# Two chunks per product in the small GLA levels of a hybrid GLA and mLSTM decoder layer on one core

## The chip, the cores and the metric

The kernel runs on one core of a Trainium2 chip. The metric is the device time of one execution in microseconds (us). Most executions of this kernel lie within some tenths of a per cent of each other. Every duration, wait and clock below is read from one profiled execution of the kernel before.

## What is computed

One decoder layer: a norm, a wide input projection, four heads of gated linear attention (GLA) beside four heads of mLSTM, a merge by sigmoid gates, an output projection, and a convolutional feed-forward network. Sequence 1024 with 16 meta tokens in front, model width 1024, float32 throughout. The change touches the scores of the GLA heads. Per head (key width 128, value width 256):

```python
def step(S, inp):
    qc, kc, vc, la = inp
    bc = jnp.cumsum(la, axis=-2)
    inter = jnp.einsum('bhtk,bhkv->bhtv', qc * jnp.exp(bc), S)
    diff = bc[:, :, :, None, :] - bc[:, :, None, :, :]
    decay = jnp.exp(jnp.where(causal[:, :, None], diff, -jnp.inf))
    scores = jnp.einsum('bhtk,bhsk,bhtsk->bhts', qc, kc, decay)
    out = inter + jnp.einsum('bhts,bhsv->bhtv', scores, vc)
```

The decay differs per key channel, so the scores are no plain product of queries and keys.

## The kernel before, in words

**Main stream.** TensorE spends the first half of the span on projections of the normed input. They are made as float32r products in three terms (high by high, high by low, low by high): `proj_cm` (L146, matmuls on L154) gives channel-major thirds of 24 matmuls with 342 to 348 columns, `proj_v` (L172, matmuls on L184 and L197) gives the values of a head in nine pieces with 256 columns. Each third or piece ends in a `yield`. The generators are run by `main` in a fixed order, slot by slot: in slot s, the gates of head s (`gate_proj`, six thirds), then keys, queries and values of head s+1 (`head_proj`, three thirds, three thirds, nine pieces), then a merge gate (`merge_gate`, three thirds). A slot has 24 yields.

**Side stream.** The attention of a head is a generator too (`gla(s)` for heads 0 to 3, `mlstm(s)` for 4 to 7). At each yield of the main stream, `advance` runs the side stream one step. So one third of a projection (some 3.8 us of TensorE) stands between two steps, and the side work of ScalarE, VectorE and GpSimd runs under it. The side generators wait in one list and are run one after the other. `small_rows` (seven steps; it makes the small vectors that the mLSTM heads need) stands behind GLA head 0 in that list. A GLA head has 23 steps. A tile scheduler then sets the exact order of instructions on each engine, so a step's instructions can stand some way ahead of the step; each engine runs its own instructions strictly in that order.

**Scores by levels.** A chunk is 128 tokens, and there are NC = 8 chunks. Pairs of a query at t and a key at s in one chunk are split by the largest block of size b (1, 2, 4, ..., 64) that separates them: s lies in the earlier half of an aligned block of 2b tokens, t in the later half. For such pairs the decay factors at the border between the halves, and one matmul makes the level. `level(b)` (L610) builds `pk`: for earlier tokens the key times exp(border - bc), for later tokens the query times exp(bc - border). VectorE does the two subtractions (L624, L625) and the query product (L628), ScalarE the exp (L626), GpSimd the key product (L627).

- Levels 32 and 64 (`scores_pair`, L567) are packed: earlier halves of two chunks in 128 columns, later halves in another 128, and one matmul of 128 by 128 serves two chunks; four matmuls a level.
- Levels 1 to 16 (`scores_later`, L580) take one matmul per chunk: all 128 tokens stationary, the 64 later tokens moving; eight matmuls of 128 by 64 a level. `copy_predicated` (L589) then writes the valid entries into `A` by a mask.
- The diagonal (`scores`, L559) is eight matmuls of 128 by 128, in the head's first step.

These products are plain float32; each shows in the trace as two matmul records, so eight matmuls are 16 records. `A` (128 by 8 by 128) then meets the values on L720; L721 adds the state's part.

**What a head ends with.** `post` (L510) scales the rows, transposes them in groups of four (`ot`, L530, and a group for the two meta rows, `otm`, L537), multiplies by the gate into the row tile `of` (L532, L538), splits it in high and low, and sends both to DRAM. It does this for two halves of the head, and `of` has one buffer: the second half's first write waits until the first half's low part has left.

**Buffers that set the order.** PSUM tiles with tag `s` have three buffers, used in turn by all side products (scores `sc`, `pre`, `ot`, `otm`, `kt`); tag `pj` has three for the projections. Gate tiles `r` have two buffers, one head's worth. Keys `k`, queries `q`, values `v` have two each. `raw_s` (small projections) shares its one buffer with `mfs`, in which GpSimd builds the masks (L365 to L369).

Of the kernel before, what the change touches and what calls it, by code (L numbers as in the profile page):

```python
# [1 line left out]

# [14 lines left out]
P = 128  # L17
# [27 lines left out]
def hybrid_kernel(ctx, tc, x, meta, norm_mix, w_in, b_in, gla_w_gate, gla_b_gate, gla_norm,  # L45
# [167 lines left out]
    def head_units(s):  # L213
        h = s % 4
        if s < 4:
            uk[s], uq[s] = u_cm(w_in, O_GK + P * h, f"gk{h}"), u_cm(w_in, O_GQ + P * h, f"gq{h}")
            if s == 0:
                uk["lr"] = U.add()
            uv[s] = u_v(O_GV + DV * h, f"gv{h}_")
        else:  # L220
            uk[s], uq[s] = u_cm(w_in, O_MK + P * h, f"mk{h}"), u_cm(w_in, O_MQ + P * h, f"mq{h}")
            uv[s] = u_v(O_MV + DV * h, f"mv{h}_")
# [7 lines left out]
    for s in range(8):  # L230
        gate_units(s)
# [127 lines left out]
    with tc.issue_after(last.ins):  # L359
        lmask = {}  # L360
        mfs = hd.tile([P, T], F32, name="mfs", tag="raw", bufs=1)
        for i, b in enumerate((16, 8, 4, 2, 1)):
            mf = mfs[:, 64 * i:64 * (i + 1)]
            half = mf.rearrange("p (n w) -> p n w", w=b)
            nc.gpsimd.memset(half, 1.0)  # L365
            nb = P // (2 * b)
            nc.gpsimd.affine_select(out=half, in_=half, compare_op=OP.is_ge, fill=0.0, base=0,
                                    pattern=[[-2 * b, nb], [0, b]], channel_multiplier=1)
            nc.gpsimd.affine_select(out=half, in_=half, compare_op=OP.is_ge, fill=0.0, base=b - 1,  # L369
                                    pattern=[[2 * b, nb], [0, b]], channel_multiplier=-1)  # L370
            mu = hd.tile([P, 64], U8, name=f"mu{b}")
            nc.vector.tensor_copy(mu, mf)
            lmask[b] = mu
        mu = hd.tile([P, P], U8, name="mu0")
        nc.vector.tensor_copy(mu, ident)
        lmask[0] = mu
        big = hd.tile([P, P], F32, name="big")
# [173 lines left out]
    def gla(s):  # L551
# [7 lines left out]
        def scores(lt, rt, b):  # L559
            for g in range(2):  # L560
                pt = ps.tile([P, 4, P], F32, name=f"sc{s}_{b}_{g}", tag="s", bufs=3)
                for i in range(4):
                    c = 4 * g + i
                    nc.tensor.matmul(pt[:, i, :], lt[:, P * c:P * (c + 1)], rt[:, P * c:P * (c + 1)], start=True, stop=True)
                nc.vector.copy_predicated(A[:, 4 * g:4 * g + 4, :], lmask[b][:, None, :].to_broadcast([P, 4, P]), pt)

        def scores_pair(pk, b):  # L567

            m = 64 // b
# [3 lines left out]
            A2 = A.rearrange("p (i c) t -> p i c t", c=2)  # L573
            for c in range(2):
                for n in range(m):
                    p0 = b * (m * c + n)
                    nc.scalar.activation(A2[2 * b * n:2 * b * n + b, :, c, 2 * b * n + b:2 * b * (n + 1)],
                                         pt[p0:p0 + b, :, p0:p0 + b], AF.Copy)

        def scores_later(pk, b):  # L580

            n = P // (2 * b)
            pt = ps.tile([P, NC, 64], F32, name=f"sc{s}_{b}", tag="s", bufs=3)
            for c in range(NC):
                l = lv(pk[:, P * c:P * (c + 1)], b)[:, :, 1, :]
                nc.tensor.matmul(pt[:, c, :], pk[:, P * c:P * (c + 1)], l, start=True, stop=True)
# [23 lines left out]
        def level(b):  # L610
            pk = wtile(f"pk{s}_{b}")
            n = SEQ // (2 * b)
            if b < 32:
# [822 lines left out]
```

## Time and profile before

| what | value |
|---|---|
| median of 3 runs | 1971.62 us (1969.85 to 1973.77) |
| the profiled execution | 1973.3 us, of which the span is 1971.4 us |
| TensorE busy with matmuls | 1936.3 us, 98% of the span |
| VectorE, ScalarE, GpSimd busy | 963.4, 744.3, 286.5 us |
| mean granted TensorE clock | 0.996 |

How to read the rows below: PE is TensorE, PEld its weight load, DVE VectorE, ACT ScalarE, POOL GpSimd, SP the engine that issues the transfers. L597 is line 597 of the program before. A timeline row gives the start in us, the duration in us (of a merged run of xN records, from the first start to the last end), the engine, line, operation, the output tile, the inputs and the shapes; in brackets the engine's idle time before it and what ended that. Matmuls are pipelined, so a record's own duration (0.32 us) is longer than the distance from one start to the next (0.16 us), and only starts tell what one costs.

### The profile page before, as it was taken

How to read it: one execution, taken by the hardware profiler on the slowest of the kernel's cores; microseconds unless marked ns; L12 is line 12 of the kernel's file. 1: busy time of each engine (PE TensorE's matmuls, PEld its weight loads, DVE VectorE, ACT ScalarE, POOL GpSimd, SP SyncE). 2: the span in 40 equal slices, each digit the busy share in tenths (PEclk: the TensorE clock that was granted, in tenths of full speed). 3: DMA queues.
4: the chain of work that ended last, by engine and by line, in shares of the span. 5: the costliest groups of instructions: out<-in, count | busy, mean ns of one | idle time of the engine just before them, and what ended most of it. 6: DMA issues, size and time to landing. Idle time of an engine off the chain costs nothing. (4 is left out here: it accounts for less than half of the span.)

```text
span 1971.4 us, 31346 instructions
## 1 busy us (share of the span) xinstructions
PE 1936.3 (98%) x13333; PEld 1854.0 (94%) x13333; DVE 963.4 (49%) x1427; ACT 744.3 (38%) x1176; POOL 286.5 (15%) x201
## 2 busy tenths in 40 slices
PE   7999999999999999999999999999999999999998
PEld 6999999999999999999999999999999999978886
DVE  6265263637535343422022446698888888710202
ACT  5145333535534343423221234544545444431211
POOL 2020020101000000000000002012222222364220
PEclk9999999999999999999999999999999999999999
DMA  4210403232234222226971433333333333487731
GB/s 152 57 33 23 100 22 95 37 70 69 61 96 90 64 88 63 79 62 123 315 268 54 150 108 108 124 102 126 116 119 123 118 118 113 170 301 263 239 101 43
DMA packets 191271, 224.82 MB, mean 114 GB/s; under 512 B 11102, under 2 KB 150640, under 8 KB 191131
## 3 DMA queue, kind: packets, MB, share of 16 engines
q1 hardware_dynamic: 190843, 221.76, 37.2%
q8 instruction: 105, 1.72, 0.4%
q10 hardware_dynamic: 288, 1.05, 0.1%
q14 instruction: 35, 0.29, 0.0%
HBM read 166.07 MB, written 56.71 MB: 113 GB/s over the span
## 5 line engine op out<-in xcount | busy, mean ns | idle before, releaser
L1323 PE MATMUL pd<-ringH,a 128*128 128x512 f32 x416 | 131.6, 393 | 1.5 <-DMA a<-adrL 1.5
L154 PE MATMUL pj<-xH,wH_r 128*128 128x342 f32 x384 | 124.2, 323 | 0.4 <-ACT r L426 0.4
L154 PE MATMUL pj<-xH,wL_r 128*128 128x342 f32 x384 | 122.9, 320 | 0.0
L154 PE MATMUL pj<-xL,wH_r 128*128 128x342 f32 x384 | 122.5, 319 | 0.0
L1357 DVE TENSOR_TENSOR acc<-pd,acc 128x512 f32<-128x512 f32 x16 | 11.1, 692 | 196.3 <-PE pd L1323 196.3
L1323 PEld LDWEIGHTS pd<-ringH,a 128*128 128x128 f32 x416 | 78.0, 188 | 19.6 <-DMA a<-adrL 2.0
L1323 PE MATMUL pd<-ringL,a 128*128 128x512 f32 x208 | 82.5, 397 | 1.5 <-POOL ringL L1302 1.5
L197 PE MATMUL pv<-wH_gv,xH 128*128 128x256 f32 x256 | 75.4, 294 | 0.0
L197 PE MATMUL pv<-wH_mv,xH 128*128 128x256 f32 x256 | 74.2, 290 | 0.0
L1193 PE MATMUL po<-wL_wo,yH 128*128 128x256 f32 x256 | 72.0, 282 | 2.0 <-DVE wL_wo L103 2.0
L1193 PE MATMUL po<-wH_wo,yH 128*128 128x256 f32 x256 | 72.8, 284 | 0.9 <-DVE h L1200 0.9
L154 PEld LDWEIGHTS pj<-xH,wH_r 128*128 128x128 f32 x384 | 72.2, 188 | 1.1 <-ACT r L426 0.5
L627 POOL TENSOR_TENSOR pk<-pk,kT 128x512 f32<-128x512 f32 x24 | 40.2, 1685 | 226.9 <-ACT pk L626 226.8
L197 PE MATMUL pv<-wL_gv,xH 128*128 128x256 f32 x256 | 72.7, 284 | 0.0
L197 PE MATMUL pv<-wH_gv,xL 128*128 128x256 f32 x256 | 72.6, 283 | 0.0
L154 PEld LDWEIGHTS pj<-xL,wH_r 128*128 128x128 f32 x384 | 72.2, 188 | 0.0
L154 PEld LDWEIGHTS pj<-xH,wL_r 128*128 128x128 f32 x384 | 72.2, 188 | 0.0
L197 PE MATMUL pv<-wL_mv,xH 128*128 128x256 f32 x256 | 71.9, 281 | 0.0
L197 PE MATMUL pv<-wH_mv,xL 128*128 128x256 f32 x256 | 71.9, 281 | 0.0
L1193 PE MATMUL po<-wH_wo,yL 128*128 128x256 f32 x256 | 71.8, 281 | 0.0
L1154 DVE SCALAR_TENSOR_TENSOR cv<-u,fc,cv 128x1024 f32<-128x1024 f32 x44 | 69.4, 1578 | 0.4
L201 DVE TENSOR_TENSOR v<-pv,bB 128x256 f32<-128x256 f32 x64 | 27.0, 421 | 78.1 <-PE pv L197 77.9
(618 smaller groups left out, 6714.5 us busy)
## 6 DMA issues: line engine op xcount, KB each, us to landing
rd<-in_ffn_w_down_dram SPq DMA_DIRECT2D x36, 512.0 KB, 5.9
rg<-in_ffn_w_up_dram SPq DMA_DIRECT2D x22, 512.0 KB, 4.2
ru<-in_ffn_w_up_dram SPq DMA_DIRECT2D x22, 512.0 KB, 3.8
a<-adrH SPq DMA_DIRECT2D x44, 256.0 KB, 5.0
a<-adrL SPq DMA_DIRECT2D x44, 256.0 KB, 4.7
adrH<-aH SPq DMA_DIRECT2D x21, 512.0 KB, 2.6
adrL<-aL SPq DMA_DIRECT2D x21, 512.0 KB, 2.6
wr_r<-in_w_in_dram SPq DMA_DIRECT2D x16, 512.0 KB, 4.0
```

Of the source, the lines that this page charges most:

```text
L154: nc.tensor.matmul(pt[:, :n], a[:, k, :], b[:, k, base + t0:base + t0 + n], start=(i == 0), stop=(i == 3 * NK - 1))
L197: nc.tensor.matmul(pt[:, :DV], a[:, k, t0:t0 + P], b[:, k % 4, :], start=(i == 0), stop=(i == 3 * NK - 1))
L201: nc.vector.tensor_tensor(vt[:n, c, :DV], pt[:n, :DV], bB[:n, :], OP.add)
L627: nc.gpsimd.tensor_tensor(pe, pe, lv(kv, b)[:, :, 0, :], OP.mult)
L1154: nc.vector.scalar_tensor_tensor(y, u[:, j:SEQ + j], fc[:, j, jj:jj + 1], y, OP.mult, OP.add)
L1193: nc.tensor.matmul(pt[:, :DV], a, b[:, k % 4, :], start=(k == 0 and i == 0), stop=(k == NK - 1 and i == len(terms) - 1))
L1323: nc.tensor.matmul(pts[t][n], a[:, c], b[:, 512 * n:512 * n + 512], start=start and i == 0, stop=stop and i == 2)
L1357: nc.vector.tensor_tensor(acc[:, h], pts[t][n], acc[:, h], OP.add)
```

## The change

- Levels 1 to 16 are packed as levels 32 and 64 are: two chunks to a matmul, four matmuls of 128 by 128 a level (`products`, `scores_small`) where eight of 128 by 64 stood. In a product of two chunks only the two diagonal quarters are wanted. So that both can be written straight over the later columns of the two chunks, the odd chunk's earlier rows are put into `pk` in mirrored order; with that, the scores of an odd chunk come out with their rows mirrored, in the same `A`.
- In `level(b)` for b under 32, the subtraction for the earlier tokens and the key product are each made in two instructions of 256 columns (even chunks; odd chunks mirrored) instead of one of 512.
- `turn` brings the odd chunks' rows back: one float32 matmul with a mirrored identity `flip` (128 by 512 columns), and one ScalarE copy into a new tile `An`. `An` takes the buffer of tag `oH`. It stands two steps behind level 16.
- The diagonal moves from the head's first step to the step of level 32's scores, behind `turn`, since `turn` overwrites whole rows. A GLA head has 24 steps: one fewer at its start, two more at level 64.
- Masks: 22 `affine_select` on GpSimd for the level masks and `flip` where 10 stood (one more, for `big`, is in both), five masks of 128 by 128 where five of 128 by 64 stood, and the tile `flip`.
- Order: for s below 5, the six thirds of keys and queries of head s+1 come ahead of the six gate thirds of head s; the weights are prepared in that order too. `small_rows` is put behind GLA head 3 instead of head 0.

```diff
+    GATE_LATER = [s < 5 for s in range(8)]
...
+        nc.gpsimd.memset(mfs[:, :P * 6], 1.0)
...
+        for i, b in enumerate((16, 8, 4, 2, 1)):
+            mf = mfs[:, P * (i + 1):P * (i + 2)]
+            nb = P // (2 * b)
+            for odd in range(2):
+                half = mf[:, 64 * odd:64 * odd + 64].rearrange("p (n w) -> p n w", w=b)
+                for base, sg in (((P - 1) * odd, -1), (b - 1 - (P - 1) * odd, 1)):
+                    nc.gpsimd.affine_select(out=half, in_=half, compare_op=OP.is_ge, fill=0.0, base=base,
...
+        def turn():
+
+            pt = ps.tile([P, 4, P], F32, name=f"sct{s}", tag="s", bufs=3)
+            nc.tensor.matmul(pt, flip, A.rearrange("p (i c) t -> p i c t", c=2)[:, :, 1, :], start=True, stop=True)
+            nc.scalar.activation(An, pt, AF.Copy)
+
+        def products(pk, b):
+
             pt = ps.tile([P, 4, P], F32, name=f"sc{s}_{b}", tag="s", bufs=3)
             for i in range(4):
                 nc.tensor.matmul(pt[:, i, :], pk[:, P * i:P * (i + 1)], pk[:, 512 + P * i:512 + P * (i + 1)], start=True, stop=True)
-            A2 = A.rearrange("p (i c) t -> p i c t", c=2)
+            return pt
...
-        def scores_later(pk, b):
-
-            n = P // (2 * b)
-            pt = ps.tile([P, NC, 64], F32, name=f"sc{s}_{b}", tag="s", bufs=3)
-            for c in range(NC):
-                l = lv(pk[:, P * c:P * (c + 1)], b)[:, :, 1, :]
-                nc.tensor.matmul(pt[:, c, :], pk[:, P * c:P * (c + 1)], l, start=True, stop=True)
-            dst = A.rearrange("p c (n h w) -> p c n h w", h=2, w=b)[:, :, :, 1, :]
-            m = lmask[b].rearrange("p (n w) -> p n w", w=b)[:, None].to_broadcast([P, NC, n, b])
-            nc.vector.copy_predicated(dst, m, pt.rearrange("p c (n w) -> p c n w", w=b))
-
-        scores(kv, qv, 0)
-        yield
+        def scores_small(pk, b):
+            pt = products(pk, b)
+            dst = A.rearrange("p (i c) (n h w) -> p i (c n) h w", c=2, h=2, w=b)[:, :, :, 1, :]
+            m = lmask[b].rearrange("p (n w) -> p n w", w=b)[:, None].to_broadcast([P, 4, P // b, b])
+            nc.vector.copy_predicated(dst, m, pt.rearrange("p i (n w) -> p i n w", w=b))
...
+                e = pk[:, :512].rearrange("p (i n h w) -> p i n h w", n=64 // b, h=2, w=b)
+                pe = [e[:, :, :, 0, :], e[:, :, ::-1, 1, ::-1]]
...
-                nc.vector.tensor_tensor(pe, ref, b4[:, :, 0, :], OP.subtract)
+                for e, _, t in early:
+                    nc.vector.tensor_tensor(e, t[..., b - 1:b].to_broadcast(t.shape), t, OP.subtract)
...
-                nc.gpsimd.tensor_tensor(pe, pe, lv(kv, b)[:, :, 0, :], OP.mult)
+                for e, k, _ in early:
+                    nc.gpsimd.tensor_tensor(e, e, k, OP.mult)
...
             if b == 64:
-                scores_pair(pk, 32)
+                yield
+                turn()
+                yield
+                scores_diagonal()
+                scores_large(pk, 32)
...
-                nc.tensor.matmul(op[:, i, :], A[:, c, :], vt[:, c + 1, :DV], start=True, stop=False)
+                nc.tensor.matmul(op[:, i, :], Ac[c], vt[:, c + 1, :DV], start=True, stop=False)
...
-        if s == 0:
+        if s == 3:
             side.append(small_rows())
+        nxt = head_proj(s + 1) if s < 7 else iter(())
+        if GATE_LATER[s]:
+            main(islice(nxt, 6))
         main(gate_proj(s))
-        if s < 7:
-            main(head_proj(s + 1))
+        main(nxt)
         main(merge_gate("a", s))
```

Three places show how the order of instructions moves. The rows name line, operation, output and inputs, and columns (or partitions by columns); xN is a run of N like instructions.

TensorE in slot 0 around level 2 of head 0 (`sc_2`); `pj` are projection matmuls, `gk`, `gq` and `r` the weights of keys, queries and gates. Before:

```order
L154 MATMUL pj_684_1181<-xL,wH_r_1_749 128x342
L154 MATMUL pj_684_1181<-xH,wL_r_1_750 128x342
L586 MATMUL sc_2_1213<-pk_2_1165 128x64 x8
L154 MATMUL pj_0_1233<-xH,wH_gk_991 128x348
L154 MATMUL pj_0_1233<-xL,wH_gk_991 128x348
```

The same place in the changed kernel:

```order
L155 MATMUL pj_342_1155<-xL,wH_gq_759 128x342
L155 MATMUL pj_342_1155<-xH,wL_gq_760 128x342
L600 MATMUL sc_2_1189<-pk_2_1141 128x128 x4
L155 MATMUL pj_684_1195<-xH,wH_gq_759 128x342
L155 MATMUL pj_684_1195<-xL,wH_gq_759 128x342
```

Four matmuls of 128 columns stand where eight of 64 stood, and they stand under the queries of head 1 and no longer at the end of the gates of head 0.

TensorE from the end of one GLA head to the start of the next: the transposes `ot` and `otm` of the rows, then the first products of the next head. Before, head 2 to head 3 (24 projection matmuls stand at each line of dots):

```order
L537 MATMUL otm_0_3968<-ident,om_3653 128x2
...
L530 MATMUL ot_1_0_4003<-ident,or_0_3687 128x128 x4
...
L530 MATMUL ot_1_1_4042<-ident,or_1_3688 128x128 x4
L537 MATMUL otm_1_4048<-ident,om_3653 128x2
...
L564 MATMUL sc_0_0_4082<-qT_3154,kT_3153 128x128 x4
L564 MATMUL sc_0_1_4088<-qT_3154,kT_3153 128x128 x4
...
L597 MATMUL pre_0_4121<-raw_s,wg 128x348
```

In the changed kernel, head 0 to head 1 (24 matmuls at each line of dots again):

```order
L555 MATMUL otm_0_1878<-ident,om_1571 128x2
...
L548 MATMUL ot_1_0_1913<-ident,or_0_1605 128x128 x4
...
L548 MATMUL ot_1_1_1945<-ident,or_1_1606 128x128 x4
L555 MATMUL otm_1_1951<-ident,om_1571 128x2
...
L623 MATMUL pre_0_1998<-raw_s,wg 128x348
L623 MATMUL pre_348_2000<-raw_s,wg 128x346
L623 MATMUL pre_694_2002<-raw_s,wg 128x346
```

The next head's first products come as far behind the last transposes as before, but they are the three `pre`, which take all three PSUM buffers at once, where the two diagonal products took two.

VectorE at that same place: `of` are the rows of the output, `wL` the low part of a weight. Before, head 1 to head 2:

```order
L541 TENSOR_TENSOR of_0_2986<-of_0_2986,oH_0_3028 128x1026
L532 SCALAR_TENSOR_TENSOR of_1_3066<-ot_1_0_3067,col,r_1_2062 128x512
L532 SCALAR_TENSOR_TENSOR of_1_3066<-ot_1_1_3099,col,r_1_2062 128x512
L538 SCALAR_TENSOR_TENSOR of_1_3066<-otm_1_3105,col,r_1_2062 128x2
L541 TENSOR_TENSOR of_1_3066<-of_1_3066,oH_1_3108 128x1026
```

In the changed kernel, head 0 to head 1:

```order
L559 TENSOR_TENSOR of_0_1832<-of_0_1832,oH_0_1881 128x1026
L550 SCALAR_TENSOR_TENSOR of_1_1912<-ot_1_0_1913,col,r_1_1352 128x512
L550 SCALAR_TENSOR_TENSOR of_1_1912<-ot_1_1_1945,col,r_1_1352 128x512
L104 TENSOR_TENSOR wL_r_0_1967<-wr_r_0_1964,wH_r_0_1966 128x1024
L556 SCALAR_TENSOR_TENSOR of_1_1912<-otm_1_1951,col,r_1_1352 128x2
L559 TENSOR_TENSOR of_1_1912<-of_1_1912,oH_1_1954 128x1026
```

A weight's low part now stands between the row transposes and the meta row of the second half, ahead of the instruction that empties the third PSUM buffer.

More of the change, by code (lines that the diff above doesn't have):

```diff
@@ L1 @@
 from contextlib import ExitStack
+from itertools import islice
 import concourse.bass as bass
@@ L211, in hybrid_kernel, with kq_units @@
     uk, uq, uv, ur, uga, ugb = {}, {}, {}, {}, {}, {}
-    def head_units(s):
+    GATE_LATER = [s < 5 for s in range(8)]
+    def kq_units(s):
+        if s in uk:
+            return
         h = s % 4
@@ L216, in head_units @@
             uk[s], uq[s] = u_cm(w_in, O_GK + P * h, f"gk{h}"), u_cm(w_in, O_GQ + P * h, f"gq{h}")
-            if s == 0:
-                uk["lr"] = U.add()
-            uv[s] = u_v(O_GV + DV * h, f"gv{h}_")
         else:
             uk[s], uq[s] = u_cm(w_in, O_MK + P * h, f"mk{h}"), u_cm(w_in, O_MQ + P * h, f"mq{h}")
-            uv[s] = u_v(O_MV + DV * h, f"mv{h}_")
+    def head_units(s):
+        h = s % 4
+        kq_units(s)
+        if s == 0:
+            uk["lr"] = U.add()
+        uv[s] = u_v((O_GV if s < 4 else O_MV) + DV * h, f"{'gm'[s // 4]}v{h}_")
     def gate_units(s):
@@ L230, in hybrid_kernel @@
     for s in range(8):
+        if GATE_LATER[s]:
+            kq_units(s + 1)
         gate_units(s)
@@ L361, in hybrid_kernel @@
         mfs = hd.tile([P, T], F32, name="mfs", tag="raw", bufs=1)
[L362 to L373, printed above, removed]
+        nc.gpsimd.memset(mfs[:, :P * 6], 1.0)
+        for sg in (1, -1):
+            nc.gpsimd.affine_select(out=mfs[:, :P], in_=mfs[:, :P], compare_op=OP.is_ge, fill=0.0, base=-sg * (P - 1),
+                                    pattern=[[sg, P]], channel_multiplier=sg)
+        flip = hd.tile([P, P], F32, name="flip")
+        nc.vector.tensor_copy(flip, mfs[:, :P])
         mu = hd.tile([P, P], U8, name="mu0")
@@ L557, in lv, with scores_diagonal @@
             return t.rearrange("p (n h w) -> p n h w", h=2, w=b)
-        def scores(lt, rt, b):
+        An = hd.tile([P, T], F32, name=f"An{s}", tag="oH", bufs=1)[:, :512].rearrange("p (i t) -> p i t", t=P)
+        Ac = [An[:, c // 2, :] if c % 2 else A[:, c, :] for c in range(NC)]
+        def scores_diagonal():
             for g in range(2):
-                pt = ps.tile([P, 4, P], F32, name=f"sc{s}_{b}_{g}", tag="s", bufs=3)
+                pt = ps.tile([P, 4, P], F32, name=f"sc{s}_0_{g}", tag="s", bufs=3)
                 for i in range(4):
[L563 to L569, printed above, removed]
+                    c = 2 * i + g
+                    nc.tensor.matmul(pt[:, i, :], kv[:, P * c:P * (c + 1)], qv[:, P * c:P * (c + 1)], start=True, stop=True)
+                nc.vector.copy_predicated(An if g else A.rearrange("p (i c) t -> p i c t", c=2)[:, :, 0, :],
+                                          lmask[0][:, None, :].to_broadcast([P, 4, P]), pt)
+        def turn():
[3 more added lines that the diff above has]
+        def products(pk, b):
             pt = ps.tile([P, 4, P], F32, name=f"sc{s}_{b}", tag="s", bufs=3)
@@ L612, in level @@
             n = SEQ // (2 * b)
+            pe, pl = (pk[:, 512 * i:512 * (i + 1)].rearrange("p (n w) -> p n w", w=b) for i in range(2))
+            src = [lv(t, b)[:, :, 0, :] for t in (kv, bcv)]
             if b < 32:
-                pv = lv(pk[:, :SEQ], b)
-                pe, pl = pv[:, :, 0, :], pv[:, :, 1, :]
-            else:
-                pe, pl = (pk[:, 512 * i:512 * (i + 1)].rearrange("p (n w) -> p n w", w=b) for i in range(2))
+                e = pk[:, :512].rearrange("p (i n h w) -> p i n h w", n=64 // b, h=2, w=b)
+                pe = [e[:, :, :, 0, :], e[:, :, ::-1, 1, ::-1]]
+                src = [[t.rearrange("p (i c n h w) -> p i c n h w", c=2, n=64 // b, h=2, w=b)[:, :, c, :, 0, :]
+                        for c in range(2)] for t in (kv, bcv)]
+            else:
+                pe, src = [pe], [[t] for t in src]
+            early = list(zip(pe, *src))
             if b == 1:
                 nc.scalar.activation(pl, lv(la[:, NM:], 1)[:, :, 1, :], AF.Exp, scale=1.0 / 16)
-                nc.gpsimd.tensor_copy(pe, lv(kv, 1)[:, :, 0, :])
+                for e, k, _ in early:
+                    nc.gpsimd.tensor_copy(e, k)
             else:
@@ L656, in gla @@
         nc.scalar.activation(dl, bl.rearrange("p n w -> p (n w)"), AF.Exp, scale=1.0 / 16)
-        scores_pair(pk, 64)
+        scores_large(pk, 64)
         yield
```

16 lines of the change are left out of this document (13 added, 3 removed).

## The prediction

> **What bounds the kernel now.** I read the page's first lines, then the table by stretches, TensorE's own waits, and the timeline of TensorE around the products that change.
>
> ```profile
> span 1971.4 us, 31346 instructions
> PE 1936.3 (98%) x13333; PEld 1854.0 (94%) x13333; DVE 963.4 (49%) x1427; ACT 744.3 (38%) x1176; POOL 286.5 (15%) x201
> ```
>
> ```profile
> 90.00:200.00 110.00, 108.45 (x737) 103.77 (x736) 61.68 (x87) 52.83 (x85) 15.91 (x10) 0.98 0.15 44
> 200.00:300.00 100.00, 100.00 (x705) 96.79 (x704) 47.58 (x69) 37.58 (x63) 10.57 (x6) 1.00 0.26 58
> 300.00:400.00 100.00, 98.69 (x682) 94.57 (x681) 47.76 (x72) 41.33 (x67) 12.23 (x10) 1.00 0.27 58
> 400.00:500.00 100.00, 99.53 (x681) 96.42 (x680) 54.10 (x77) 48.51 (x80) 12.49 (x12) 1.00 0.33 76
> ```
>
> These are the four stretches in which the GLA heads run (columns: stretch, length, then busy time of PE, PEld, DVE, ACT, POOL, granted clock, DMA share, GB/s). TensorE is busy all but 3.3 us of 410, at a granted clock of 0.98 to 1.00. VectorE is at about half. So here the time is what TensorE must do, and an instruction taken from TensorE shortens the span by what it displaces, unless a wait takes its place. TensorE's waits between 40 and 920 us are these four, 3.2 us in all:
>
> ```profile
> PE ot L530 <- DVE or L520: 1.6, 1, 1.6
> PE sc L564 <- DVE of L532: 0.6, 2, 0.5
> PE otm L537 <- DVE of L538: 0.6, 1, 0.6
> PE pj L154 <- ACT r L426: 0.4, 1, 0.4
> ```
>
> **Part 1: eight narrow products become four wide ones.** What a block costs is the distance from the last projection matmul ahead of it to the second one behind it, less two ordinary steps from one projection matmul to the next start (0.15 us from 110.01 and 0.16 us from 137.95 in the rows below; 0.157 us taken). A narrow level, then a packed one (level 32, which has the very shape that levels 1 to 16 get):
>
> ```profile
> 110.01 0.32 PE L154 MATMUL pj<-xH,wL_r 128*128 128x342 f32 x1
> 110.16 1.90 PE L586 MATMUL sc<-pk 128*128 128x64 f32 x16
> 111.87 0.40 PE L154 MATMUL pj<-xH,wH_r 128*128 128x342 f32 x1
> 112.11 0.32 PE L154 MATMUL pj<-xL,wH_r 128*128 128x342 f32 x1
> ```
>
> ```profile
> 137.95 0.32 PE L154 MATMUL pj<-xH,wL_gq 128*128 128x342 f32 x1
> 138.11 1.05 PE L572 MATMUL sc<-pk 128*128 128x128 f32 x8
> 138.92 0.40 PE L154 MATMUL pj<-xH,wH_gq 128*128 128x342 f32 x1
> 139.16 0.32 PE L154 MATMUL pj<-xL,wH_gq 128*128 128x342 f32 x1
> ```
>
> Narrow: 112.11 - 110.01 = 2.10 us. Packed: 139.16 - 137.95 = 1.21 us. The difference is 0.89 us a level. The 16 narrow records start 0.107 us apart (1.71 / 16), the 8 wide ones 0.101 us (0.81 / 8): a record of 64 columns costs as much as one of 128. With 5 levels in 4 heads, 20 x 0.89 = **-17.8 us**.
>
> [...]
>
> **Part 2: `turn`.** One float32 matmul of 512 columns a head, so two records, 1024 columns to stream. No record of before has 512 columns in float32. The nearest are `pre` (six records, 348 columns at most) and `op` (two records of 256 columns to each start below):
>
> ```profile
> 96.57 0.32 PE L154 MATMUL pj<-xH,wL_r 128*128 128x342 f32 x1
> 96.82 2.01 PE L597 MATMUL pre<-raw_s,wg 17*128 17x348 f32 x6
> 98.76 0.42 PE L154 MATMUL pj<-xH,wH_r 128*128 128x342 f32 x1
> 99.02 0.32 PE L154 MATMUL pj<-xL,wH_r 128*128 128x342 f32 x1
> ```
>
> ```profile
> 157.24 0.59 PE L721 MATMUL op<-S,qh 128*128 128x256 f32 x2
> 157.67 0.59 PE L720 MATMUL op<-v,A 128*128 128x256 f32 x2
> ```
>
> `op`: 0.43 us for 512 columns, 0.84 ns a column, so 0.86 us a turn. `pre`, with entry and exit: 99.02 - 96.57 - 0.31 = 2.14 us for 2080 columns (348 + 346 + 346, twice), 1.03 ns a column, 1.05 us a turn. I take 1.0, near the row that stands alone among projections as `turn` will: **+4.0 us** for four heads (3.4 to 4.2). Its ScalarE copy (a copy of 512 columns from PSUM) lies under the next third.
>
> **Part 3: the diagonal.** Its matmuls stay. It now stands in one block with level 32, so one entry and exit less: 1.21 - 0.31 - 0.81 = 0.09 us a head, **-0.4 us**.
>
> **Part 4: work for the other engines.** Two subtractions and two key products of 256 columns replace one each of 512, a little more VectorE and GpSimd time for the second instruction's start. The room for it shrinks: a step of third and level lasted 3.77 + 1.79 = 5.6 us, and now lasts 4.7. What covers it is the lead that VectorE has over TensorE:
>
> ```profile
> 110.78 3.71 POOL L627 TENSOR_TENSOR pk<-pk,kT 128x512 f32<-128x512 f32 x2 [50.93 <-ACT pk L626]
> ```
>
> ```profile
> 110.73 0.69 DVE L628 TENSOR_TENSOR pk<-pk,qT 128x512 f32<-128x512 f32 x1
> 111.34 2.01 DVE L624 TENSOR_TENSOR pk<-bc 128x512 f32<-128x512 f32 x1
> ```
>
> Level 1's product starts at 110.16. GpSimd has the keys of levels 2 and 4 done by 114.5, 4.3 us later; with steps of 4.7 us their products are due 4.7 and 9.3 us later. Level 2's keys are done about halfway, 2.5 us behind 110.16, so 2 us are left for the second instructions. I take zero; if the cover went, see the third rival.
>
> **Part 5: masks.** GpSimd's selects are needed by `raw_s`, which shares their buffer, and behind `raw_s` stands its ScalarE copy:
>
> ```profile
> 29.40 0.82 POOL L367 TENSOR_SCALAR_AFFINE_SELECT mfs<-mfs 128x64 f32<-128x64 f32 x3
> 33.18 2.02 POOL L369 TENSOR_SCALAR_AFFINE_SELECT mfs<-mfs 128x64 f32<-128x64 f32 x2
> 37.27 0.49 ACT L403 ACTIVATE raw_s<-pj,bsm 96x272 f32<-96x272 f32 x1
> 42.73 0.28 PE L154 MATMUL pj<-xH,wH_lr 128*128 128x256 f32 x1
> ```
>
> The old masks end at 35.2. Twelve more selects at 0.27 us (0.82 / 3) end them near 39, at 1 us each near 47. TensorE wants that PSUM buffer again at 42.73. I take zero, with up to 4 us for the slow end.
>
> **Part 6: the order, and the waits.** The wait of `ot` (1.6 us) came as `small_rows` was run by VectorE between the last products of head 0 and the scaling of its rows; it goes from head 0 to head 3 with `small_rows`, and costs the same there. The other three lie where one head's rows are still being written: the second half's first write waits for the first half's transfer, and holds the PSUM buffers that the next head's first products want.
>
> ```profile
> 433.96 0.22 PE L537 MATMUL otm<-ident,om 2*128 2x2 f32 x1
> ```
>
> ```profile
> 438.00 0.60 PE L530 MATMUL ot<-ident,or 128*128 128x128 f32 x4
> ```
>
> ```profile
> 324.54 0.22 PE L537 MATMUL otm<-ident,om 2*128 2x2 f32 x1
> ```
>
> ```profile
> 338.32 1.41 DVE L532 SCALAR_TENSOR_TENSOR of<-ot,col,r 128x512 f32<-128x512 f32 x2 [7.94 <-DMA oscgL<-of]
> ```
>
> ```profile
> 439.13 1.22 DVE L103 TENSOR_TENSOR wL_mq<-wr_mq,wH_mq 128x1024 fp32r<-128x1024 f32 x1 [0.89 <-ACT wH_mq L102]
> 446.55 1.41 DVE L532 SCALAR_TENSOR_TENSOR of<-ot,col,r 128x512 f32<-128x512 f32 x2 [6.20 <-DMA oscgL<-of]
> 447.87 0.21 DVE L538 SCALAR_TENSOR_TENSOR of<-otm,col,r 128x2 f32<-128x2 f32 x1
> ```
>
> In head 2 the writes begin 446.55 - 433.96 = 12.6 us behind the first `otm`. The next head's products come three thirds (72 matmuls at 0.157 us or a little more, 11.4 us) and two blocks of transposes (0.6 us each) behind it, 12.6 us. Before, two buffers were wanted there; now `pre` wants three, 0.7 us apart (2.14 / 3). The third is emptied only when the two row writes (1.41), a weight's low part (1.22) and the meta row (0.2) are through: 12.6 + 2.8 = 15.4 us, where it is wanted at 12.6 + 1.4 = 14.0. That is 1.4 us, less if the copy ahead of the transfer, which no longer stands behind gate evictions, comes sooner, and more if the transfer lands as late as behind head 1 (338.32, which is 13.8 us behind its `otm` at 324.54, or 1.2 us later than here). I take 1.0 us at each of three heads: waits of 1.6 + 3.0 = 4.6 where 3.2 were, **+1.4 us**. The ends are -1.6 (none at the three heads) and 3 x (1.4 + 1.2) - 1.6 = +6.
>
> The moved keys, queries and gates are the same matmuls, 12 thirds in another order; they cost nothing on TensorE. Their weights' transfers move with them on SP's queue, each two units ahead as before.
>
> **Sum.** -17.8 + 4.0 - 0.4 + 1.4 = -12.8 us. The profiled execution took 1973.3 us (span 1971.4), the median is 1971.62. 1971.6 - 12.8 = **1958.8 us**. With the bounds of parts 2 and 6 alone: -17.8 + 3.4 - 0.4 - 1.6 = -16.4 to -17.8 + 4.2 - 0.4 + 6.0 = -8.0, so 1955 to 1964.
>
> **Rivals.**
>
> *The output rows hold the next head (slower).* Behind head 0 the same write came far later than 12.6 us:
>
> ```profile
> 189.62 0.22 PE L537 MATMUL otm<-ident,om 2*128 2x2 f32 x1
> ```
>
> ```profile
> 207.22 1.41 DVE L532 SCALAR_TENSOR_TENSOR of<-ot,col,r 128x512 f32<-128x512 f32 x2 [8.66 <-DMA oscgL<-of]
> ```
>
> That is 17.6 us. At that size the third buffer comes at 20.4 us where it is wanted at 14.0: 6.4 us at each of three heads, 19.2 us, and -17.8 + 4.0 - 0.4 + 19.2 + 1.6 - 3.2 = +3.4, 1975; with the transfers 0.5 us later still, +4.9, 1976.5. It decides from about 17.8 us on. For it: the wait stands in every head. Against it: `small_rows` lengthened that one, and it now stands behind head 3, where no GLA head follows. As slow as this: 0.03. Halfway, 1964 to 1968: 0.08.
>
> *Narrow records cost half, and nothing is gained (slower).* If columns were what counts, parts 1 and 3 give 0, and +4.0 + 1.4 are left: 1977. Both kinds stand in this trace at the same price, 0.107 and 0.101 us; 0.02.
>
> *The halved instructions hold the levels (no change, or little gain).* A subtraction took 0.69 us by itself and 2.01 us beside GpSimd's key product (rows of part 4). If each half cost what the whole did beside the other engine, a level would take VectorE 2 x 2.0 us for the halves and 0.7 us each for the other three instructions, 6.1 us against 4.7: 1.4 us for each of the five levels less 2 us of lead, 5 us a head, 20 us. Half of that is likelier where it comes at all, as the halves have half the columns: 1969. [...] 0.05.
>
> *No new waits.* If the waits at the heads' seams go, -16.4 or a little more: 1953 to 1955; 0.07.
>
> **Numbers.** The forecast (1955 to 1964) has 0.75, the rest as above. A difference of 0.2%, 3.9 us, is about what a measurement of this kernel can tell from none. Faster by more: 0.75 + 0.07 + 0.08 + 0.01 of the third rival = 0.91. Within: 0.04 of the third rival. Slower: 0.03 + 0.02 = 0.05. The range leaves out half of the halfway case and half of the last rival, and takes 1 us for the measurement: 1954 to 1965, about 8 in 10.
>
> **What would show it.** Right: 160 records of 128 columns for levels 1 to 16, with 0.81 us from a block's first start to the next projection; eight records of 512 columns for the turn, about 0.9 us a pair; TensorE's waits between 40 and 920 us at 2 to 8 us, at `pre` behind VectorE's `of`, and at `ot` of head 3. Wrong: a wait of several us at `pre` in each head, a wait of `sc` behind GpSimd's `pk`, or wide records that start more than 0.12 us apart.

## The result, and the profile after

The changed kernel took 1962.18 us (median of four runs, 1958.78 to 1962.51), the kernel before 1971.43 us beside it: a ratio of 0.9946 (95% interval 0.9933 to 0.9958), 10.7 us less. The forecast was 1958.8 us, with a range of 1954 to 1965. The profiled execution took 1962.3 us, and its span is 10.8 us shorter than before's.

The page's first lines of the changed kernel:

```profile
span 1960.6 us, 31110 instructions
PE 1925.3 (98%) x13181; PEld 1840.3 (94%) x13181; DVE 965.9 (49%) x1444; ACT 753.4 (38%) x1183; POOL 308.1 (16%) x229
```

TensorE has 152 records fewer and 11.0 us less busy time; GpSimd has 21.6 us more. The stretches of the GLA heads, and one behind them (columns as in the prediction):

```profile
90.00:200.00 110.00, 109.50 (x737) 104.14 (x736) 53.63 (x85) 47.54 (x82) 17.85 (x13) 1.00 0.19 55
400.00:500.00 100.00, 99.65 (x663) 94.62 (x662) 50.94 (x71) 49.71 (x79) 15.98 (x16) 1.00 0.22 64
500.00:560.00 60.00, 56.73 (x359) 55.59 (x359) 34.97 (x55) 28.85 (x37) 3.89 (x2) 0.94 0.42 117
```

The idle time that stood in head 0 is gone from there, and in the last row TensorE is 3.3 us idle and has a granted clock of 0.94. TensorE's waits between 40 and 920 us:

```profile
PE ot L548 <- DVE or L538: 3.2, 1, 3.2
PE sc L600 <- POOL pk L663: 0.5, 1, 0.5
PE sct L593 <- DVE A L617: 0.3, 1, 0.3
```

They are 4.0 us where 3.2 were. The two waits at the heads' seams and the one for the gate tile are gone, none at `pre` came, and the wait of `ot` has moved to head 3 and doubled.

**What a block costs now.** A small level and a turn in head 0, on TensorE's timeline:

```profile
118.54 0.32 PE L155 MATMUL pj<-xH,wL_r 128*128 128x342 f32 x1
118.70 1.05 PE L600 MATMUL sc<-pk 128*128 128x128 f32 x8
119.51 0.40 PE L155 MATMUL pj<-xH,wH_r 128*128 128x342 f32 x1
119.75 0.32 PE L155 MATMUL pj<-xL,wH_r 128*128 128x342 f32 x1
...
131.68 0.32 PE L155 MATMUL pj<-xH,wL_r 128*128 128x342 f32 x1
131.84 1.02 PE L593 MATMUL sct<-A,flip 128*128 128x512 f32 x2
132.29 0.72 PE L155 MATMUL pj<-xH,wH_r 128*128 128x342 f32 x1
132.85 0.32 PE L155 MATMUL pj<-xL,wH_r 128*128 128x342 f32 x1
```

The level: 119.75 - 118.54 = 1.21 us, as the prediction worked it out from level 32. The turn: 132.85 - 131.68 - 0.31 = 0.86 us. Of the 20 small levels the 16 of sizes 1, 4, 8 and 16 stand at 1.20 to 1.22 us; level 2 stands at 1.97, 1.51, 1.48 and 1.40 us in heads 0 to 3, for GpSimd's keys come late there. The turn of head 3 stands 0.6 us over the others. Why the keys come late is seen on GpSimd and VectorE, here in head 1:

```profile
213.13 3.19 POOL L663 TENSOR_TENSOR pk<-pk,kT 128x256 f32<-128x256 f32 x1 [35.59 <-issue]
214.83 0.75 DVE L659 TENSOR_TENSOR pk<-bc 128x256 f32<-128x256 f32 x2
```

The first half of level 2's key product takes 3.19 us, where the median half takes 1.19. It ends 0.74 us behind the last of six VectorE instructions (subtractions and a query product, L659, L660 and L664), which run from 212.96 to 215.58 without a gap. In heads 0, 2 and 3 it ends 0.73 or 0.74 us behind such a run too; in head 0 the run is longer, and the half takes 5.03 us.

**The wait at the end of head 3.** GpSimd's power (`rs3r`, the rows' norm) is what VectorE's row scaling (L538) needs, and that is what `ot` needs. VectorE and GpSimd there:

```profile
504.70 2.32 DVE L482 TENSOR_TENSOR_SCAN sr<-rmask,sr 4x1040 f32<-4x1040 f32 x1
504.82 3.79 POOL L93 TENSOR_TENSOR rs3r<-rs3v,mhalf 128x9 f32<-128x9 f32 x1 [7.21 <-DVE rs3v L91]
508.64 0.88 DVE L538 TENSOR_SCALAR or<-or,rs3r 128x256 f32<-128x256 f32 x3 [1.62 <-POOL rs3r L93]
```

The same instruction behind head 0, where no scan of `small_rows` stands beside it any more, in the profile's row for it:

```profile
L93 POOL TENSOR_TENSOR rs0r<-rs0v,mhalf x1: 1812/1812/1812, 174.9 to 174.9; 128x9 f32<-128x9 f32 x1
```

3.79 us beside the scan, 1.81 us without it. Before, the power behind head 0 had the same scan beside it and took 3.82 us, so this was there to be read. In head 3 it also started later: TensorE wants `ot` 1.1 us behind the power's start (505.9), where before it wanted it 2.7 us behind (182.2 against 179.5). The scan was beside the power before too, so this later start, 1.6 us, is what made the wait longer. These are the rows behind it:

```profile
495.15 1.28 ACT L474 ACT_TABLE_LOAD   x1
504.17 0.42 DVE L202 TENSOR_TENSOR v<-pv,bB 128x256 f32<-128x256 f32 x1
```

On VectorE two instructions of `small_rows`, one that starts at 500.56 and a first scan, stand ahead of the norm that the power needs, and they wait for ScalarE. From ScalarE's last copy but one of `op` to the first of them are 7.7 us here (492.90 to 500.56) and were 6.4 us before (169.22 to 175.58): ScalarE has a table load of 1.28 us ahead of its exp that was not there behind head 0. And the copy of a value piece out of PSUM, at 504.17, stands between that first scan and the norm, 0.3 us. TensorE at that place:

```profile
505.62 0.28 PE L198 MATMUL pv<-wH_mv,xL 128*128 128x256 f32 x1
509.05 1.59 PE L548 MATMUL ot<-ident,or 128*128 128x128 f32 x4 [3.15 <-DVE or L538]
510.29 0.63 PE L155 MATMUL pj<-xH,wH_ga 128*128 128x342 f32 x1
510.72 0.49 PE L155 MATMUL pj<-xL,wH_ga 128*128 128x342 f32 x1
511.01 0.49 PE L155 MATMUL pj<-xH,wL_ga 128*128 128x342 f32 x1
```

Behind the wait the projection matmuls start 0.29 us apart, where 0.157 is usual. The table by stretches of 2 us shows why (granted clock is the third number from the end):

```profile
506.00:508.00 2.00, 0.00 (x0) 0.00 (x0) 1.02 (x1) 1.97 (x2) 2.00 (x1) 1.00 0.00 0
508.00:510.00 2.00, 0.95 (x3) 0.55 (x3) 1.36 (x5) 1.98 (x2) 0.60 (x1) 0.54 0.00 0
510.00:512.00 2.00, 1.88 (x8) 1.84 (x8) 1.97 (x7) 1.10 (x2) 0.00 (x0) 0.50 0.00 0
512.00:514.00 2.00, 2.00 (x9) 2.00 (x8) 1.97 (x4) 0.00 (x0) 0.00 (x0) 0.50 0.00 0
514.00:516.00 2.00, 2.00 (x12) 2.00 (x11) 2.00 (x3) 0.00 (x0) 0.00 (x0) 0.75 0.19 52
```

The clock stood at one half for 4 x (0.46 + 0.50 + 0.50 + 0.25) = 6.8 us, the first part of it while TensorE was still idle. Before, behind the wait of head 0:

```profile
184.00:186.00 2.00, 2.00 (x14) 1.72 (x14) 2.00 (x8) 0.00 (x0) 0.00 (x0) 0.89 0.00 0
186.00:188.00 2.00, 2.00 (x11) 2.00 (x11) 1.87 (x4) 1.06 (x1) 0.00 (x0) 0.50 0.03 8
188.00:190.00 2.00, 2.00 (x13) 1.81 (x13) 1.97 (x4) 0.71 (x1) 0.00 (x0) 0.76 0.00 0
```

Here it was 4 x (0.11 + 0.50 + 0.24) = 3.4 us at half clock. What a wait cost in all is read from starts, from the last projection matmul ahead of it to the second block of transposes. After: 505.62 to 516.27, 10.65 us; the same records take 4.33 us in experiment 3 (505.00 to 509.34), where nothing waits, so the wait cost 6.3 us. Before: 181.94 to 189.09, 7.15 us, against 3.40 us in experiment 2 (181.78 to 185.17): 3.75 us. The 6.3 us are those of this one execution. In experiments 5 to 8 and 11, which have the same wait, only 3.4 us at half clock followed, and the stretch took 9.8 to 10.0 us: 5.5 to 5.7 us.

### The profile page after: what moved, and what is told of

It is laid out like the page before. It is cut to its first block, busy times and chain, and to the rows that moved or that the text cites. A ratio compares the mean times of both kernels' runs of the same rounds, so it can differ in the third digit from the quotient of the medians.

```text
span 1960.6 us, 31110 instructions
## 1 busy us (share of the span) xinstructions
PE 1925.3 (98%) x13181; PEld 1840.3 (94%) x13181; DVE 965.9 (49%) x1444; ACT 753.4 (38%) x1183; POOL 308.1 (16%) x229
## 3 DMA queue, kind: packets, MB, share of 16 engines
q8 instruction: 103, 1.69, 0.4%
## 5 line engine op out<-in xcount | busy, mean ns | idle before, releaser
L663 POOL TENSOR_TENSOR pk<-pk,kT 128x256 f32<-128x256 f32 (+1 forms) x40 | 58.8, 1501 | 163.0 <-ACT pk L661 90.5
L202 DVE TENSOR_TENSOR v<-pv,bB 128x256 f32<-128x256 f32 x64 | 26.8, 420 | 87.3 <-PE pv L198 87.3
```

Of the source, the lines that this page charges most:

```text
L202: nc.vector.tensor_tensor(vt[:n, c, :DV], pt[:n, :DV], bB[:n, :], OP.add)
L663: nc.gpsimd.tensor_tensor(e, e, k, OP.mult)
```

## The experiments

Each run is compared with runs of the kernel before on the same chip; the ratios are to those, with their 95% intervals. The changed kernel's own ratio was 0.9946, and 0.9938 when it was measured again (experiment 11).

The theory from the two traces: the packing is worth what the prediction said, and the missing microseconds lie in the wait of head 3 with its half clock. The rival: the order costs nothing and the packing is worth less. Each experiment's text names the two as they bear on it.

**1. The packing without the order.**

```diff
-    GATE_LATER = [s < 5 for s in range(8)]
+    GATE_LATER = [False] * 8
...
-        if s == 3:
+        if s == 0:
             side.append(small_rows())
```

> The packing without the order: the gates stay ahead of the next keys and queries, and the small rows stay behind head 0. Theory A (the packing is worth 17.8 - 3.4 for the turn + 0.4, about 14.7 us, and the 10.7 us of the whole change are less because TensorE's wait at the end of head 3 costs 3.2 us of idleness and then several us of half clock): the wait of head 0 stays as it was, so 1971.4 - 14.7 = 1957, and up to 1961 if the next head's first gate products wait about 1 us at three heads. Theory B (the order is free, and the packing itself brings only 10.7 us): 1961 and no such waits.

Measured: 1979.7 us, ratio 1.0034 (1.0022 to 1.0046), slower than before. Both theories failed. Its largest waits of TensorE between 40 and 920 us:

```profile
PE sct L593 <- DVE A L617: 5.2, 3, 2.0
PE ot L548 <- DVE of L550: 3.3, 5, 1.1
PE pj L155 <- ACT r L444: 3.1, 3, 1.4
PE ot L548 <- DVE or L538: 2.9, 2, 1.6
```

All of them sum to 15.7 us, and three stretches at half clock (3.4, 3.4 and 6.8 us) lie in the same part. The turn waits for VectorE, which is behind with the masked copies, in heads 1 to 3 and not in head 0.

**2. The order without the packing**: the edits of the diff at `GATE_LATER`, the slots and `small_rows`, made in the kernel before.

> The order without the packing: the scores as before, the keys and queries ahead of the gates, the small rows behind head 3. Theory A: the wait behind head 3 (3.2 us, then half clock for 6.8 us) takes the place of that behind head 0 (1.6 us, then half clock for 3.4 us), 6.5 us instead of 3.3 us: +3 us, less up to 1.6 us for the three waits at the heads' seams that go: 1973 to 1974.5. Theory B (the order is free): 1970 to 1971.5.

Measured: 1973.9 us, ratio 1.0005 (0.9996 to 1.0013): within the measurement of no change, and at the edge of both expectations. The three small waits are gone and one of 3.4 us at `ot` of head 3 is left, with 6.8 us of half clock behind it. So the packing alone loses 6.6 us, the order alone brings nothing that can be told from the measurement, and both together bring 10.7 us. The parts don't add up, and the next question is what the order gives to the packing.

**3. The small rows later**: their first instructions on ScalarE and VectorE wait in their own queues until head 3's squares and row scaling are issued.

```diff
-        nc.scalar.activation(e, f, AF.Abs)
+        with tc.issue_after(ends["sq"].ins):
+            nc.scalar.activation(e, f, AF.Abs)
...
+        with tc.issue_after(ends["rows"].ins):
+            nc.vector.scalar_tensor_tensor(lf, f, 0.0, e, OP.min, OP.subtract)
...
```

> The changed kernel, but the first instructions of the small rows on ScalarE and VectorE are put behind head 3's last squares and its row scaling. Theory A: GpSimd's power takes 1.8 us and not 3.8, TensorE's wait at head 3 goes or falls under 1 us, and with it the half clock: 1962.2 - 6.5 + 0.5 = 1956 (1955 to 1958). Theory B (a wait costs only its idle time): 1962.2 - 3.2 = 1959. If the small rows then come too late for the first mLSTM head, a new wait shows there and the time stays at 1962 or above.

Measured: 1955.8 us, ratio 0.9910 (0.9897 to 0.9923); by the ratios that is 5.5 to 7.1 us under the changed kernel (0.9938 and 0.9946). The waits of TensorE that are left between 40 and 920 us:

```profile
PE sc L605 <- POOL pk L668: 0.5, 1, 0.5
PE sct L598 <- DVE A L622: 0.4, 1, 0.4
```

The wait at `ot` is gone, and the clock stands at 1.00 from 500 to 560 us. A wait that cost only its idle time would have given 1959, and the times alone barely tell the two apart, at intervals of 2.5 us either way. The trace tells it: the stretch across the old wait takes 4.33 us instead of 10.65, 6.3 us less, of which 3.2 were idle. Theory A's price holds, but its way there does not. The power did not fall to 1.8 us:

```profile
499.60 2.82 POOL L93 TENSOR_TENSOR rs3r<-rs3v,mhalf 128x9 f32<-128x9 f32 x1 [3.09 <-DVE rs3v L91]
```

It took 2.82 us, beside `kc` on VectorE, and the wait went because it began 5.7 us ahead of TensorE's need for `ot` (499.6 against 505.3) and not 1.1. So 4.6 us of lead came from the earlier start and 1.0 us from the shorter power.

**4. The small rows behind head 0**, with keys and queries still ahead of the gates (the second edit of experiment 1 alone).

> The changed kernel, but with the small rows behind head 0, as before the change; keys and queries stay ahead of the gates. Theory A: a wait of 1.6 us and 3.4 us of half clock behind head 0 in place of 3.2 us and 6.8 us behind head 3: 1962.2 - 3.3 = 1959. The prediction's first rival (the output rows, held up by the small rows, hold the next head's gate products): a wait of up to 6 us at the first products of head 1: 1965.

Measured: 1968.2 us, ratio 0.9973 (0.9963 to 0.9983). Neither theory: no wait at `pre` of head 1, but 4.7 us at the turns of heads 1 to 3, 1.4 us at a score product behind the turn's copy, and 1.5 us at `ot` (1.3 us more in three small ones).

From 1 and 4 I formed another theory. `small_rows` takes seven steps of the side stream. Behind head 0 they slide heads 1 to 3 against the main stream, so that part of the small levels stands under value pieces (2.9 us of TensorE) and no longer under projection thirds (3.8 us). Narrow levels filled up the difference; packed ones don't. Experiments 5 and 9 try this.

**5. The gates first, the small rows behind head 3** (the first edit of experiment 1 alone).

> The changed kernel with the gates of a head ahead of the next head's keys and queries, as before the change; the small rows stay behind head 3. Theory A (it is the small rows' place that keeps the levels under projection thirds, since seven or eight steps behind head 0 slide heads 1 to 3 under the shorter value pieces): the levels lie under thirds here too, no wait of the turn for VectorE, and the time is that of the changed kernel within 2 us, 1960 to 1964. Theory B (the order of the gates is what counts): waits of the projections for the gate tiles and of the turn, 8 us or more, 1970 and above.

Measured: 1960.7 us, ratio 0.9932 (0.9919 to 0.9946). Theory A: the place of the small rows is what the packing needs. With them behind head 3, the place of the gates can't be told from nothing; with them behind head 0 it was worth 11.5 us (experiments 1 and 4): waits of 15.7 against 8.9 us, and 13.7 against 3.4 us at half clock.

**6. Quarter products on GpSimd.**

```diff
                 for e, k, _ in early:
-                    nc.gpsimd.tensor_tensor(e, e, k, OP.mult)
+                    for u in ([e, k],) if b >= 32 else ([t[:, :2] for t in (e, k)], [t[:, 2:] for t in (e, k)]):
+                        nc.gpsimd.tensor_tensor(u[0], u[0], u[1], OP.mult)
```

> The changed kernel with each of GpSimd's half key products of levels 2 to 16 made in two instructions of 128 columns. Theory A (GpSimd has room: the halves take 3 us of a step of 4.7 us, and an instruction's cost goes mostly by its columns, so that four take 3.0 to 4 us): no change, 1962, one wait of a score product for GpSimd of 0.5 to 1.5 us in head 0. Theory B (an instruction costs much the same whatever its columns, so four take about 5.6 us): GpSimd becomes the bound of the levels, 0.9 us at each of four levels in four heads less the lead, +8 to +14: 1970 to 1976.

Measured: 1962.4 us, ratio 0.9944 (0.9930 to 0.9958): no change. Their group, with the mean of one in ns:

```profile
L664 POOL TENSOR_TENSOR pk<-pk,kT 128x128 f32<-128x128 f32 x64 | 56.0, 911 | 151.1 <-ACT pk L661 79.8 <-issue 71.4
```

A quarter takes 0.91 us, a half 1.44 us in the changed kernel, a whole 1.69 us before; these means include the few that VectorE held up. Four quarters are 3.6 us of a step of 4.7 us, and GpSimd still has room.

**7. The turn twice.**

```diff
...
                 turn()
+                turn_idle()
                 yield
```

`turn_idle` makes the same matmul and the same copy as `turn`, with a PSUM tile of its own (`scu`).

> The changed kernel with the turn's matmul and its ScalarE copy made twice. Theory A (what the changed kernel's timeline shows, 0.86 us a turn): 4 x 0.86 less an entry and exit, +3 to +3.5: 1965.5. The prediction's price of 1.0 us: +4: 1966.2. If the copy or a wait holds the turn, more than that.

Measured: 1966.2 us, ratio 0.9964 (0.9952 to 0.9977), 4.0 us over the first median of the changed kernel. The two prices lie too near each other for the time to tell them apart. The timeline does:

```profile
132.31 1.02 PE L593 MATMUL sct<-A,flip 128*128 128x512 f32 x2
133.17 1.02 PE L598 MATMUL scu<-A,flip 128*128 128x512 f32 x2
```

The second starts 0.86 us behind the first.

**8. Half the columns.** The products of levels 1 to 16 move 64 columns each. The scores of the later tokens of odd chunks are left out, and the masked copy is made in two instructions (not shown below).

```diff
-            pt = products(pk, b)
+            pt = ps.tile([P, 4, P], F32, name=f"sc{s}_{b}", tag="s", bufs=3)
+            for i in range(4):
+                nc.tensor.matmul(pt[:, i, :64], pk[:, P * i:P * (i + 1)], pk[:, 512 + P * i:576 + P * i], start=True, stop=True)
...
```

> The changed kernel, but each product of levels 1 to 16 moves only 64 of its 128 columns; the scores of the later tokens of odd chunks are left out (the even chunks' stand in their place), and the masked copy is made in two instructions. Theory A (a record costs its weight load, not its columns: 0.101 against 0.107 us): no change, 1962, or 1 to 3 us more for the split copies. Theory B (columns count): 160 records at half of 0.1 us are 8 us less, 1954.

Measured: 1962.8 us, ratio 0.9944 (0.9930 to 0.9957): no change. In the timeline:

```profile
104.45 1.00 PE L616 MATMUL sc<-pk 128*128 128x64 f32 x8
105.26 0.40 PE L155 MATMUL pj<-xH,wH_gq 128*128 128x342 f32 x1
```

Eight records of 64 columns take 0.81 us, as eight of 128 did. Part 1 of the prediction rests on this, and it holds: a record of 64 columns took what one of 128 took, 0.101 us (0.81 / 8) from start to start. That the weight load sets it is not shown, for no run varies the load.

**9. The slide alone.** Seven empty steps behind head 0; the small rows stay behind head 3.

```diff
+    def idle_steps():
+        for _ in range(7):
+            yield
...
+        if s == 0:
+            side.append(idle_steps())
```

> The changed kernel with seven empty steps of the side stream behind head 0, where the small rows' seven steps stood before the change; the small rows themselves stay behind head 3. Theory A (the slide alone puts the small levels of heads 1 to 3 under the value pieces, whose steps are too short for VectorE's work): the waits of the run with the small rows behind head 0 come back, 4 to 5 us at the turn and 1 to 2 us at score products, with or without half clock, and the time is 5 to 10 us above the changed kernel's: 1967 to 1972. Theory B (the small rows' own work on VectorE and ScalarE made those waits): 1962.

Measured: 1964.8 us, ratio 0.9954 (0.9941 to 0.9968), 3.5 us over the changed kernel on the same chip (experiment 11). The waits came back without any work of the small rows:

```profile
PE sct L593 <- DVE A L617: 4.0, 3, 1.4
PE ot L548 <- DVE of L550: 1.4, 2, 1.1
PE sc L600 <- ACT An L594: 1.4, 1, 1.4
```

With three of 0.5 to 0.6 us they sum to 8.5 us. The time is less than theory A gave, for the wait of `ot` in head 3 shrank from 3.2 to 0.6 us (head 3 slid too, to a place under thirds), and no half clock followed any of these waits. Nor is the slide all of what experiment 4 lost: that run is 3.7 us above this one by the ratios (0.9973 against 0.9954), with the work of the small rows behind head 0 too. The small levels of head 1 in this run, and the stretch that holds them:

```profile
249.43 1.05 PE L600 MATMUL sc<-pk 128*128 128x128 f32 x8
253.16 1.05 PE L600 MATMUL sc<-pk 128*128 128x128 f32 x8
261.24 1.13 PE L593 MATMUL sct<-A,flip 128*128 128x512 f32 x2 [1.34 <-DVE A L617]
```

```profile
238.00:262.00 24.00, 22.59 (x180) 21.82 (x178) 24.00 (x36) 10.68 (x13) 12.79 (x10) 1.00 0.09 23
```

And in the changed kernel:

```profile
221.99 1.05 PE L600 MATMUL sc<-pk 128*128 128x128 f32 x8
226.66 1.05 PE L600 MATMUL sc<-pk 128*128 128x128 f32 x8
```

```profile
208.00:240.00 32.00, 31.97 (x214) 31.67 (x213) 29.78 (x38) 16.44 (x23) 14.50 (x10) 1.00 0.13 34
```

A step is 3.73 us here and 4.67 us there. VectorE (third pair of numbers) is busy in all 24.0 us of the first stretch, and 29.8 of 32 us in the second: under the value pieces it is the bound, and under the thirds it just isn't. The shorter cover is not the whole of it. A packed level asks 3.65 us of VectorE in this run (two subtractions for the earlier tokens 0.97, one for the later 0.78, query product 0.95, masked copy 0.95), which 3.73 us would still cover; but VectorE also takes each value piece out of PSUM (0.41 us at L202), while a third is taken out by ScalarE. Together 4.06 us. Before, a narrow level under a value piece made a step of 4.6 us (258.29 to 262.92 for levels of head 1), so the slide did no harm there.

**10. Both better places together**: experiments 3 and 5 in one.

> The small rows put behind head 3's row scaling, and the gates again ahead of the next keys and queries: the two edits that by themselves took 6.4 us and 1.5 us off the changed kernel. If both hold together: 1954 to 1955. If the second was within the measurement, 1955 to 1956. If the late small rows need the gates' later place, a wait of 1 us or more behind head 3 shows, 1957 to 1960.

Measured: 1954.7 us, ratio 0.9904 (0.9889 to 0.9919), the shortest of all; one wait of 0.2 us is left between 40 and 920 us. Against experiment 3 alone (0.9910) the difference is within the measurement.

**11. The changed kernel again**, beside 9 and 10.

> The changed kernel once more, beside the two others on one chip: 1962, with TensorE's wait of 3.2 us behind head 3 and a half clock of 3.4 or 6.8 us behind it.

Measured: 1961.3 us, ratio 0.9938 (0.9926 to 0.9950). The wait at `ot` is there, with 3.4 us of half clock this time. Experiment 10 is 6.6 us under it on the same chip.

## Why the prediction was right, and where it missed

The mechanism was right for the kernel as changed: TensorE is the bound, a record of 64 columns costs what one of 128 does (0.107 and 0.101 us from start to start before), and eight records fewer a level are worth 0.89 us. The forecast was 3.4 us too low, and by span 2.0 us. That it came so near is in part luck, for several of its parts missed and the misses cancel. By its own parts:

- **Part 1** held: -17.8 us, 1.20 to 1.22 us a block in 16 of 20 levels, and experiment 8 shows the premise (0.81 us for eight records of 64 columns, as for eight of 128).
- **Part 2**: 0.86 us a turn, so +3.4 and not +4.0; of its two rows the one of `op` was right. A wait in head 3, 0.6 us that the prediction did not have, makes it +4.0 again, by luck.
- **Part 3**: the joint block of diagonal and level 32 takes 3.00 us, which is what the two took apart (2.10 + 1.21 - 0.31). 0, not -0.4.
- **Part 4**, taken at zero, costs 1.5 us: level 2's four blocks over 1.21 us (0.76 + 0.30 + 0.27 + 0.19). The prediction gave level 2's keys 2.5 us and 2 us to spare. They took 4.0 us in heads 1 to 3 and 5.8 us in head 0 (103.32 to 109.17), as their first half ended only 0.73 to 0.74 us behind VectorE's run (3.19 us in head 1, where the median half took 1.19). The prediction's third rival also has one engine slower beside the other, but there it is VectorE (2.01 us against 0.69); in level 2 it was GpSimd. The rest of GpSimd's cover is real (experiment 6). VectorE's cover was worked out in head 0 alone. That it held in heads 1 to 3 too was luck: it hung on `small_rows` leaving head 0, which the prediction did not see.
- **Part 5** held: GpSimd's selects end at 38.9 us, and nothing waits for them.
- **Part 6** failed in the step "it goes from head 0 to head 3 with `small_rows`, and costs the same there". It cost 6.3 us in the profiled execution and 5.5 to 5.7 us in five others, and 3.75 us before. What stands ahead of the power behind head 3 is not what stood behind head 0: a table load on ScalarE and a value's copy on VectorE put it off by 1.6 us, with the scan beside it as before. Experiment 3 takes all of it away. The prediction also counted waits by their idle time alone; it had the clock of 0.98 in its own row for 90 to 200 us and gave it no term. And the three waits of 1.0 us at `pre` did not come: the second half's first write now comes 9.0 us behind the first `otm` (195.03 against 186.00 us in head 0) and not 12.6. In head 2 before, the low part's transfer was issued 4.3 us behind `otm` and its buffer was free 8.3 us later; after, 3.4 and 5.8 us. The prediction named the first as possible; that the transfer itself is shorter is shown, its cause is only argued (no weight's transfer is issued in those microseconds).

So part 6 came to 2.6 - 2.2 = +0.4 us, by a longer wait and lost ones, where +1.4 was forecast; parts 2 to 4 came to +5.5 us where +3.6 was.

The sum up to the end of the heads, from blocks and waits: -17.8 + 1.5 + 4.0 + 2.6 for `ot` (6.3 less 3.75), and -2.2 for the waits at the old seams (2.54 and 2.83 us for two diagonals where 2.10 is usual, 0.6 at `otm`, 0.4 at `pj`), is -11.9; a first stage that ended 0.8 us earlier (86.42 against 87.24 us at the transpose `ftp`; its cause stays open) makes it -12.7. The first `bg` product, behind all heads, starts at 963.65 us where it started at 976.54: -12.9. The other 0.2 us stay open. Then 2.1 us are given back in stages that the change doesn't touch. Most of it is at one wait of 2.2 us (`Y` for ScalarE's `BH1t`) that is in both kernels: after it the clock fell in the profiled execution of the changed kernel (granted 0.83 from 1270 to 1280 us) and not in that of before (1.00 at the same place), 1.7 us. This is chance: the clock fell behind this wait in 8 of the 13 traces.

Of the rivals, "the halved instructions hold the levels" had the right engine, VectorE, for the waits of experiments 1, 4 and 9, but not its condition. It is not the instructions' number that decides (two half subtractions take 0.99 us where a whole one took 0.95), it is what TensorE work a level stands under (steps of 3.73 us in head 1 of experiment 9, of 4.67 us in the changed kernel). The prediction called the moved order free. On TensorE it is; but with the old order the packing loses 6.6 us (experiment 1) where it now gains 10.7, and with `small_rows` alone left behind head 0 it gains 4.9 (experiment 4).

## What to carry to other kernels

An instruction stream that is made shorter on the bounding engine also takes away the cover of the others: work out each step's new length against the work that must fit under it, at every place where the step occurs, and not only at the one that the trace shows best. A block that sits in a queue of steps has a price in slots, apart from its work: seven steps of a side job shifted three heads under shorter covers (2.9 us of TensorE where 3.8 stood). A block that moves also meets new neighbours on every engine, so price it at its new place and not at its old one. And a wait on TensorE is worth its idle time and the half clock that can follow (here 3.15 us of idle time cost 6.3 us), so look at the granted clock behind each wait before pricing it.

## What the runs showed of the hardware

- **The clock after a wait.** All changes of the granted clock in a trace lie on one grid of 3.41 us, in each of the 13 traces: before, at 185.56 and 188.97 us, one step apart; in the changed kernel, at 508.17, 515.00, 1272.76 and 1276.17 us, which are 2, 222 and 1 steps apart. A spell at half clock behind a wait lasted 3.4 us or twice that. Whether it came went with TensorE's idle time inside one step of that grid. Between 40 and 1900 us, half clock followed in 14 of 14 steps with more than 1.9 us of idle time, in 9 of 35 with 1.5 to 1.9 us, and in 1 of 48 with 1.0 to 1.5 us. Before, 1.55 us inside one step had it behind them (head 0), while 1.53 and 1.61 us in later steps of the same trace had none. The grid lies elsewhere in each trace, and the same wait had different prices: the 3.15 us at `ot` of head 3 fell on two steps with 2.27 and 0.88 us in the changed kernel (6.8 us at half clock followed), with 1.81 and 1.34 us in experiment 5 (3.4 us). In experiment 4 a wait of 1.55 us had none behind it, and the stretch across it took 6.55 us where 4.32 is usual, so it cost 0.7 us more than its idle time even so.
- **GpSimd's power beside a scan.** 128 by 9 elements took 1.81 us alone (head 0 of the changed kernel), 3.79 us beside a VectorE scan of 2.32 us (head 3), and 2.82 us beside VectorE's `kc` (experiment 3).
- **GpSimd's key products beside VectorE.** 128 columns took 0.91 us in the mean (experiment 6), 256 and 512 columns 1.19 us (changed kernel) and 1.75 us (before) at the median, so two halves cost 0.6 us more than one whole. In the changed kernel the first half of level 2 began inside a run of VectorE instructions, one behind the other without a gap, and ended only 0.73 to 0.74 us behind the run: it took 3.19 to 3.23 us in three heads, 5.03 us in one. In those three heads the next three halves took 0.86 to 1.19 us, and there a subtraction of VectorE (L660) took 1.21 us, where 0.68 stood beside the first half.
